# Eight high halves before eight low ones in mixer B, and weight units split in four half-width steps

## The chip, the cores and the metric

The kernel runs on one core of one Trainium2 chip. The metric is the device time of one execution in microseconds (us); the median of three runs of the kernel before is 1575.03 us (1574.35 to 1576.03). Engines are named as in the profile: PE is the matrix array (TensorE), PEld its weight loader, DVE is VectorE, ACT is ScalarE, POOL is GpSimd, SP is the engine that issues most of the DMAs. L12 is line 12 of the kernel before.

## The reference, cut to what matters

Two layers over 1024 tokens of width 1024. Layer 0 has mixer A, attention over a neighbourhood of the token grid; layer 1 has mixer B, grouped-query attention over all tokens. Each layer then projects, adds, and adds a gated per-layer embedding. All of it is float32.

```python
def mixer_b(h, w_in, q_norm_g, k_norm_g, w_out):
    proj = h @ w_in
    q, k, v, gate = jnp.split(proj, [...], axis=-1)
    q = rms_norm(q.reshape(b, s, 16, 64), q_norm_g); k = rms_norm(k.reshape(b, s, 4, 64), k_norm_g)
    q, k = rope(q), rope(k)
    ...
        sc = jnp.einsum('bkgqd,bksd->bkgqs', qb, k) * scale
        pr = jax.nn.softmax(sc, axis=-1)
        return jnp.einsum('bkgqs,bksd->bkgqd', pr, v)     # the products with v
    ...
    return (o * jax.nn.silu(gate)) @ w_out
```

Mixer A has 16 heads; each query there attends to a window of 8 x 16 keys with a relative bias.

## The kernel before, in words

**Numbers in two halves.** Each float32 operand of a product is kept as a high half in the array's reduced format (`fp32r`) and a low half, the rest. A projection takes three products for each 128-row piece: high with high, high with low, low with high (`split3`, L303, recorded at L301 like all matmuls). For v, high and low halves of its 64 columns lie side by side in one 128-column tile `V`, so a product with `V` gives both, and the transposed probabilities come as `PTh` and `PTl`.

**The order of the work** is written out by hand. Mixer A runs head by head, eight steps of 128 queries in each; mixer B runs 128 steps of 128 queries (head, half, t) in four groups of 32. In mixer B a step has the scores (`f_S`: four matmuls, then a minimum on DVE, L1054), the exponential (`f_E`: ACT, L1060), the transposition (`f_T`: twice four transposes on PE, L1070, each four into one PSUM bank `t`; ACT writes `PTh`, L1072, then DVE writes `PTl`, L1073, which frees the bank) and, on every second step, the products with v (`f_AV`, L1078). `psT` has two banks, so the transposes of one step need both `PTl` of the step before. `PTh` and `PTl` each hold two steps (256 columns), and `f_AV` multiplies the eight key blocks of both into a bank `o`, 16 matmuls of 128x256:

```python
                for k in range(NT):
                    v = V[h // 4][:, k]
                    mm(o, v, PTh[:, k], t == 1 and k == 0, False)
                    mm(o, v, PTl[:, k], False, t == 3 and k == NT - 1)
```

In the order of emission `f_AV` of one step stands behind the scores and a projection piece or two and ahead of the next transposition. Mixer A has its own `f_AV` (L676), in which high and low also alternate; the change leaves it alone.

**`mix`** (L334) weaves two lists: the attention items, and `dense` items (pieces of the projections for the next head or group, of the gates, and of the per-layer embedding). After each attention item it calls `pulse`, which is one `WQ.pump()` and one tick of `post`, a list of small steps with due times counted in pulses (for instance the evacuation of `o`, L478 and L442, and the norms of q and k, L313 to L323). Dense items then follow as their share of the cost comes due; they call no pulse.

**The weights** come in 92 units of 128x1024 float32 (`Weights`, L176; the queue is `WQ`). `stage` (L193) issues the load of a unit on SP into one of two `wstage` buffers, two units ahead of the split, and not before `lag` = 3 pumps after the last split. `pump` (L205) takes a unit that has been staged for `age` = 3 pumps, if its pool has room, and splits it: ACT copies the unit to the high half (L216), and DVE subtracts to get the low half (L217). The low half is not emitted at once but kept in `rest`; the next `pump`, or the next `get` of any unit by a dense item, emits it through `settle` (L223). `get` (L228) also splits by force if the unit asked for isn't there yet. ACT, DVE, POOL and SP each execute in the order of emission.

In mixer A the table of relative biases of the next head (`table`, L620) is loaded by SP into `u` (L622), and POOL works on it (L625) ahead of the y products (L512, L513); ACT then makes their high half (L509).

Of the kernel before, what the change touches and what calls it, by code (L numbers as in the profile page):

```python
# [15 lines left out]
AF = mybir.ActivationFunctionType  # L16
ALU = mybir.AluOpType
# [4 lines left out]
NT = 8  # L22
# [131 lines left out]
def trunk(ctx, tc, x, wts, rpb, gains, hgains, mask, rope, out):  # L154
    nc = tc.nc
    sync, act, dve, pool, pe = nc.sync, nc.scalar, nc.vector, nc.gpsimd, nc.tensor
# [19 lines left out]
    class Weights:  # L176
        def __init__(self):
            self.q = []
            self.staged = 0
            self.split = 0  # L180
            self.st = {}
            self.live = {1: 0, 2: 0, 3: 0}
            self.cap = {1: WSLOTS, 2: 0, 3: 0}
            self.alloc = {1: lambda: [wp1.tile([128, 1024], F32R, name=f"w{c}1") for c in "hl"]}
            self.clock = 0
            self.tiles = {}
            self.hold = None
            self.age = AGE
            self.lag = LAG
            self.last = -9  # L190
            self.rest = None

        def stage(self, force=False):  # L193
            if not force and self.clock - self.last < self.lag:
# [9 lines left out]

        def pump(self, force=False):  # L205
            self.clock += 1
            self.settle()
            self.stage(force)
            if self.split >= self.staged:
                return  # L210
            key, pid = self.q[self.split]
            if self.live[pid] >= self.cap[pid] or not (force or self.clock - self.st[key][1] >= self.age):
                return
            s, _ = self.st.pop(key)
            hi, lo = self.alloc[pid]()
            act.activation(hi, s, AF.Copy)  # L216
            self.rest = lambda: dve.tensor_tensor(lo, s, hi, ALU.subtract)  # L217
            self.tiles[key] = (hi, lo, pid)
            self.live[pid] += 1
            self.split += 1  # L220
            self.last = self.clock

        def settle(self):  # L223
            if self.rest:
                self.rest()
                self.rest = None

        def get(self, key):  # L228
            self.settle()
# [12 lines left out]
    WQ = Weights()  # L242
# [57 lines left out]
    def mm(ps, a, b, first, last):  # L300
        pe.matmul(ps, a, b, start=first, stop=last, skip_group_check=True)  # L301
# [251 lines left out]
    def mixer_a():  # L553
        with ExitStack() as es:
# [7 lines left out]
            V = one.tile([128, NT, 4, 128], F32R, name="V")  # L562
# [92 lines left out]
            def f_E(h, j):  # L655
                k0, k1 = near(j)
                n = (k1 - k0 + 1) * 128
                sp, mn = SP[h, j]
                act.activation(sp[:, :n], sp[:, :n], AF.Exp, bias=mn, scale=-1.0, accum_out=RS[h][:, j:j + 1])
# [123 lines left out]
            PTh = ptp.tile([128, NT * 3, 128], F32R, name="PTh")  # L783
            PTl = ptp.tile([128, NT * 3, 128], F32R, name="PTl")
# [14 lines left out]
            def av_and_v(h, kb):  # L799
                fs = [(lambda: f_AV(h, kb), CA[4])]  # L800
                if h % 4 == 3 and h < NH - 1:
                    fs += [(f, 0.0) for f in v_items(h // 4 + 1, kb)]
                return fs

            for h in range(NH):
                att = []
                for j in range(NT):
                    n = h * NT + j
                    def head(h=h, j=j):
                        later.tick()  # L810
                        if j == 1 and h + 1 < NH:
                            table(h + 1)
                    att.append((head, CA[0]))
                    att.append((lambda h=h, j=j: f_T(h, j), CA[1]))
                    if n + 1 < len(steps):
                        att.append((lambda n=n: f_E(*steps[n + 1]), CA[2]))
                    if n + 2 < len(steps):
                        att.append((lambda n=n: f_S(*steps[n + 2]), CA[3]))
                    if n >= 2:
                        att += av_and_v(*steps[n - 2])  # L820
                    if h == 15 and j >= YLOAD_A:
                        for t in ((j - YLOAD_A,) if j < NT - 1 else range(j - YLOAD_A, NT)):
                            att.append((lambda t=t: load_y(0, t), 0.0))
                    if h == 14 and j == OPEN3:
                        att.append((open3, 0.0))
                if h == NH - 1:
                    att += [(lambda: f_AV(NH - 1, NT - 2), CA[4]), (lambda: f_AV(NH - 1, NT - 1), CA[4])]
                dense = []
                if h < NH - 1:
                    dense += qk_items(h + 1)  # L830
                p = h // 2
                if h < 14:
                    dense += gate_items("ag", p, h % 2, dalloc, sb, gg)
                elif h == 14:
                    dense += gate_items("ag", 7, 0, dalloc, sb, gg) + gate_items("ag", 7, 1, dalloc, sb, gg)
                else:
                    dense += pp_items(0, dalloc, sb, TAGS_A)
                mix(att, dense, 4 if h == 0 else 0, HOLD if h == NH - 1 else 0)
            post.flush()
            later.flush()  # L840
            WQ.cap[3] = 0

    def mixer_b(pend):
        with ExitStack() as es:
# [10 lines left out]
            PTh = one.tile([128, NT, 256], F32R, name="PTh")  # L855
            PTl = one.tile([128, NT, 256], F32R, name="PTl")
# [9 lines left out]
            KA, KB, V, QT, QST, P, RS, OP = {}, {}, {}, {}, {}, {}, {}, {}  # L866
# [211 lines left out]
            def f_AV(h, hf, t):  # L1078
                if t == 1:
                    OP[h, hf] = psO.tile([128, 512], F32, name="o")  # L1080
                o = OP[h, hf][:, (t - 1) * 128:(t + 1) * 128]
                for k in range(NT):
                    v = V[h // 4][:, k]
                    mm(o, v, PTh[:, k], t == 1 and k == 0, False)
                    mm(o, v, PTl[:, k], False, t == 3 and k == NT - 1)
                if t == 3:
                    fin = head_end(sb, h, hf, RS[h, hf], OP.pop((h, hf)), ylive, 1, gg, talloc)
                    if fin:
                        later.add(FIN[1], fin)
# [9 lines left out]
            for i, d in enumerate(pre):  # L1099
# [4 lines left out]
                d[0]()  # L1104
                pulse()
            pro[0] = False
            for g in range(4):
                att = []
                for n in range(32 * g, 32 * g + 32):
                    h, hf, t = steps[n]  # L1110
                    av = n >= 2 and n % 2 == 0
                    w = CB if av else CN
                    att.append((later.tick, w[0]))
                    if av:
                        att.append((lambda n=n: f_AV(*steps[n - 1]), w[1]))
                    te = [(lambda n=n: f_T(*steps[n]), w[2])]
                    if n + 1 < len(steps):
                        te.append((lambda n=n: f_E(*steps[n + 1]), w[3]))
                    if n % 2 == 0:
                        te.reverse()  # L1120
                    att += te
                    if n + 2 < len(steps):
                        att.append((lambda n=n: f_S(*steps[n + 2]), w[4]))
                    m = n + QS_AT
                    if m % 8 == 0 and m < len(steps):
                        hn, fn, _ = steps[m]
                        att.append((lambda hn=hn, fn=fn: q_stack(hn // 2, fn), 0.0))
                    if YLOAD_B <= n < YLOAD_B + NT:
                        att.append((lambda t=n - YLOAD_B: load_y(1, t), 0.0))
                if g == 3:  # L1130
                    att.append((lambda: f_AV(*steps[-1]), CB[1]))
                def gates(p):
                    return [i for hf in range(2) for i in gate_items("bg", p, hf, dalloc, sb, gg)]
                dense = []
                if g > 0:
                    dense += left
                if g < 3:
                    qi = q_items(g + 1, pool)
                    kv = kv_items(1, pool) if g == 1 else [None, None]
                    dense += kv[:-2] + qi[:KS] + [k for k in kv[-2:-1] if k] + qi[KS:8] + [k for k in kv[-1:] if k] + gates(2 * g + 1) + qi[8:]  # L1140
                    left = gates(2 * g + 2)
                else:
                    WQ.cap[3] = 2
                    dense += gates(2 * g + 1) + pp_items(1, dalloc, sb, TAGS_B)
                mix(att, dense, hold=HOLD if g == 3 else 0)
            post.flush()
            later.flush()
            WQ.cap[3] = 0

    def dense_phase(l):  # L1150
# [164 lines left out]
```

## Time and profile before

| what | value |
| --- | --- |
| median of three runs | 1575.03 us (1574.35 to 1576.03) |
| the profiled execution, its own time | 1577.5 us |
| its span, first to last instruction | 1575.6 us |
| PE, PEld, DVE, ACT, POOL busy | 1523.6, 1328.7, 1023.9, 871.4, 269.5 us |
| mean granted clock of the array | 0.997 |

The busy times come from the profile's first part. In its groups of instructions a row gives line, engine, operation, tiles, shape, count, then busy time, mean duration in ns of one, and the engine's idle time before them with what ended it. A row of waits gives who waited, for whom, and total, number and longest in us. A row of the busy time by stage gives the stretch in us from the span's start, its length, then busy time and count for PE, PEld, DVE, ACT and POOL, the granted clock, the busy share of the DMA engines, and GB/s. A row of the timeline gives start and duration in us. Matmuls overlap, so their pace is read from one start to the next and not from their durations. A row of the chain that ended last gives start, duration, and what the end then hung on.

### The profile page before, as it was taken

The numbers are of one execution on the slowest core, as the hardware profiler recorded it, in microseconds if no ns is written. First come the engines' busy times: TensorE is split into PE (matmuls) and PEld (weight loads), VectorE is DVE, ScalarE is ACT, GpSimd is POOL, SyncE is SP. The second block draws the span as 40 slices with busy tenths as digits, with TensorE's granted clock in tenths as the row PEclk, the third lists the DMA queues.
The fourth block names the chain that finished last, engine by engine and source line by source line (L and its number), as shares of the span: only waits on it lengthen the run. The fifth ranks groups of instructions, "written<-read, shape, count | busy, mean of one in ns | idle before, by whom it ended". The sixth has DMA issues, their size and how long they took to land.

```text
span 1575.6 us, 24284 instructions
## 1 busy us (share of the span) xinstructions
PE 1523.6 (97%) x9048; PEld 1328.7 (84%) x9048; DVE 1023.9 (65%) x2062; ACT 871.4 (55%) x1744; POOL 269.5 (17%) x372
## 2 busy tenths in 40 slices
PE   6999999999999999999999999999999999999997
PEld 5888988988988788888988889989899888778886
DVE  6566576376467435648877786777777877525636
ACT  6465465366366622433467676766667767622422
POOL 2102102112022010000222132443131200000023
PEclk9999999999999999999999999999999999999999
DMA  8212122132122972142210111102111213651213
GB/s 272 78 45 65 53 80 78 39 92 78 39 79 77 343 257 68 54 140 94 74 49 21 38 51 41 58 24 65 39 32 43 74 41 112 223 201 54 71 55 129
DMA packets 89861, 138.84 MB, mean 88 GB/s; under 512 B 16912, under 2 KB 55952, under 8 KB 89744
## 3 DMA queue, kind: packets, MB, share of 16 engines
q1 hardware_dynamic: 85136, 122.62, 23.8%
q10 hardware_dynamic: 4608, 14.68, 2.6%
q8 instruction: 71, 1.16, 0.3%
q14 instruction: 46, 0.38, 0.1%
HBM read 104.65 MB, written 36.15 MB: 89 GB/s over the span
## 4 chain that ended last, share of the span: by engine, by line
PE 41%; DVE 7%; ACT 3%; issue 2%; ACTq 0%; DVEq 0%
PE d L301 21%; PE o L301 8%; PE t L1070 5%; PE s L301 5%; DVE PTl L1073 2%; DVE mn L1054 1%; ACT PTh L1072 1%; DVE wl L217 1%; PE t L426 1%; ACT wh L216 1%; PE t L1024 0%; ACT P L1060 0%; DVE QS L1034 0%; DVE ss L901 0%; DVE KB L965 0%
## 5 line engine op out<-in xcount | busy, mean ns | idle before, releaser
L301 PE MATMUL d<-wh,HTh 128*128 128x256 f32 (+1 forms) x1096 | 372.3, 340 | 5.0 <-ACT HTh L427 2.3
L301 PE MATMUL d<-wh,HTl 128*128 128x256 f32 (+1 forms) x1096 | 365.8, 334 | 1.5 <-DVE HTl L428 1.5
L301 PE MATMUL d<-wl,HTh 128*128 128x256 f32 (+1 forms) x1096 | 365.2, 333 | 0.0
L1073 DVE TENSOR_TENSOR PTl<-t,PTh 128x512 fp32r<-128x512 f32 x256 | 164.4, 683 | 114.8 <-ACT PTh L1072 114.4
L301 PEld LDWEIGHTS d<-wh,HTh 128*128 128x128 f32 x1096 | 207.7, 189 | 28.3 <-ACT HTh L427 2.9
L301 PEld LDWEIGHTS d<-wh,HTl 128*128 128x128 f32 x1096 | 207.7, 189 | 24.1 <-DVE HTl L428 2.2
L301 PEld LDWEIGHTS d<-wl,HTh 128*128 128x128 f32 x1096 | 208.0, 190 | 21.6
L301 PE MATMUL d<-HTh,wh 128*128 128x512 f32 x504 | 205.9, 409 | 0.0
L301 PE MATMUL d<-HTh,wl 128*128 128x512 f32 x504 | 197.8, 392 | 0.0
L301 PE MATMUL d<-HTl,wh 128*128 128x512 f32 x504 | 197.5, 392 | 0.0
L1060 ACT ACTIVATE P<-s,mn 128x1024 f32<-128x1024 f32 x128 | 142.7, 1114 | 66.6 <-DVE mn L1054 65.7
L301 PE MATMUL o<-PTl,V 128*128 128x256 f32 (+2 forms) x672 | 175.6, 292 | 3.3 <-DVE PTl L1073 2.2
L301 PE MATMUL o<-PTh,V 128*128 128x256 f32 (+2 forms) x672 | 174.2, 289 | 2.6 <-ACT P L1060 1.1
L1072 ACT ACTIVATE PTh<-t 128x512 fp32r<-128x512 f32 x256 | 139.4, 592 | 44.9 <-PE t L1070 44.3
L1054 DVE TENSOR_REDUCE mn<-s 128x1 f32<-128x1024 f32 x128 | 154.7, 1209 | 10.9 <-PE s L301 10.8
L1070 PE MATMUL t<-ident,P 128*128 128x128 f32 x1024 | 136.9, 275 | 7.6 <-DVE PTl L1073 6.1
L217 DVE TENSOR_TENSOR wl<-wstage,wh 128x1024 fp32r<-128x1024 f32 x89 | 113.8, 1284 | 40.8 <-ACT wh L216 40.3
L301 PEld LDWEIGHTS o<-PTl,V 128*128 128x128 f32 x672 | 128.9, 192 | 10.7 <-DVE PTl L1073 6.5
L301 PEld LDWEIGHTS o<-PTh,V 128*128 128x128 f32 x672 | 128.7, 192 | 8.3 <-issue 1.5
L1070 PEld LDWEIGHTS t<-ident,P 128*128 128x128 f32 x1024 | 115.0, 140 | 22.2 <-DVE PTl L1073 15.6
L301 PE MATMUL s<-KA,QS 128*128 128x512 f32 (+2 forms) x384 | 133.6, 402 | 0.0
L301 PE MATMUL s<-KB,QS 128*128 128x512 f32 (+2 forms) x384 | 121.8, 371 | 0.0
(178 smaller groups left out, 2436.9 us busy)
## 6 DMA issues: line engine op xcount, KB each, us to landing
wstage<-in_wts SPq DMA_DIRECT2D x92, 512.0 KB
X<-in_x SPq DMA_DIRECT2D x16, 512.0 KB
pp<-ppD SPq DMA_DIRECT2D x32, 256.0 KB
rb<-rD SPq DMA_DIRECT2D x56, 128.0 KB
ppD<-th SPq DMA_DIRECT2D x24, 256.0 KB
xD<-X SPq DMA_DIRECT2D x8, 512.0 KB
X<-xD SPq DMA_DIRECT2D x8, 512.0 KB
yD0h<-rb SPq DMA_DIRECT2D x14, 256.0 KB
```

Of the source, the lines that this page charges most:

```text
L216: act.activation(hi, s, AF.Copy)
L217: self.rest = lambda: dve.tensor_tensor(lo, s, hi, ALU.subtract)
L301: pe.matmul(ps, a, b, start=first, stop=last, skip_group_check=True)
L426: pe.transpose(ps[:, k], xn[:, (4 * c + k) * 128:(4 * c + k + 1) * 128], ident)
L1054: dve.tensor_reduce(mn, ps, axis=AX.X, op=ALU.min)
L1060: act.activation(p, ps, AF.Exp, bias=mn, scale=-1.0, accum_out=RS[h, hf][:, t:t + 1])
L1070: pe.transpose(ps[:, i], p[:, k * 128:(k + 1) * 128], ident)
L1072: act.activation(PTh[:, ks, c], ps, AF.Copy)
L1073: dve.tensor_tensor(PTl[:, ks, c], ps, PTh[:, ks, c], ALU.subtract)
```

## The change

Two edits. In mixer B's `f_AV` the eight products with `PTh` come first, then the eight with `PTl`. And while `WQ.fine` is set, which it is during the main loops of both mixers, `pump` splits a unit that isn't forced in four steps: high half of columns 0 to 511, high half of columns 512 to 1023 (both ACT), then the two low halves (both DVE). The first step is emitted at once; each later `pump` emits one step and returns, without staging a load and without splitting another unit until none is left. A `get` by a dense item still emits all steps that are left. Outside the main loops the split stays as it was.

```diff
         def pump(self, force=False):
             self.clock += 1
+            if self.fine and self.rest:
+                self.settle(1)
+                return
             self.settle()
             self.stage(force)
...
             hi, lo = self.alloc[pid]()
-            act.activation(hi, s, AF.Copy)
-            self.rest = lambda: dve.tensor_tensor(lo, s, hi, ALU.subtract)
+            ws = (slice(0, 512), slice(512, 1024)) if self.fine and not force else (slice(0, 1024),)
+            for w in ws:
+                self.rest.append(lambda w=w: act.activation(hi[:, w], s[:, w], AF.Copy))
+            for w in ws:
+                self.rest.append(lambda w=w: dve.tensor_tensor(lo[:, w], s[:, w], hi[:, w], ALU.subtract))
+            self.settle(1)
...
-        def settle(self):
-            if self.rest:
-                self.rest()
-                self.rest = None
+        def settle(self, n=9):
+            while self.rest and n:
+                self.rest.pop(0)()
+                n -= 1
...
# mixer_a, ahead of its loop over heads, and mixer_b, ahead of its loop over groups
+            WQ.fine = True
...
# both, behind that loop
             post.flush()
             later.flush()
+            WQ.settle()
+            WQ.fine = False
...
# mixer_b, f_AV
                 for k in range(NT):
-                    v = V[h // 4][:, k]
-                    mm(o, v, PTh[:, k], t == 1 and k == 0, False)
-                    mm(o, v, PTl[:, k], False, t == 3 and k == NT - 1)
+                    mm(o, V[h // 4][:, k], PTh[:, k], t == 1 and k == 0, False)
+                for k in range(NT):
+                    mm(o, V[h // 4][:, k], PTl[:, k], False, t == 3 and k == NT - 1)
```

More of the change, by code (lines that the diff above doesn't have):

```diff
@@ L190, in __init__ @@
             self.last = -9
-            self.rest = None
+            self.rest = []
+            self.fine = False
         def stage(self, force=False):
@@ L221, in pump @@
             self.last = self.clock
-        def settle(self):
-            if self.rest:
-                self.rest()
-                self.rest = None
+        def settle(self, n=9):
+            while self.rest and n:
+                self.rest.pop(0)()
+                n -= 1
         def get(self, key):
@@ L1106, in mixer_b @@
             pro[0] = False
+            WQ.fine = True
             for g in range(4):
@@ L1147, in mixer_b @@
             later.flush()
+            WQ.settle()
+            WQ.fine = False
             WQ.cap[3] = 0
```

## The prediction

> **What bounds the kernel now.** I read the page first, then the busy time by stage, then the waits inside mixer B's loop, then single places on the timeline and the chain that ended last.
>
> ```profile
> span 1575.6 us, 24284 instructions
> PE 1523.6 (97%) x9048; PEld 1328.7 (84%) x9048; DVE 1023.9 (65%) x2062; ACT 871.4 (55%) x1744; POOL 269.5 (17%) x372
> 85.00:546.00 461.00, 453.08 (x2595) 395.75 (x2594) 282.85 (x640) 268.15 (x595) 72.73 (x96) 1.00 0.27 86
> 800.00:1382.00 582.00, 565.29 (x3825) 505.96 (x3823) 430.59 (x686) 406.92 (x755) 135.52 (x213) 1.00 0.19 60
> ```
>
> The last two rows are mixer A's loop and mixer B's loop (length; then busy time of PE, PEld, DVE, ACT, POOL). The matrix array is busy in 98% of A's loop and 97% of B's. So only time in which the array stands still can be won: 461.0 - 453.1 = 7.9 us in A, 582.0 - 565.3 = 16.7 us in B. VectorE (DVE) and ScalarE (ACT) have room on average (74% and 70% in B), so they hurt by lateness at a place and not by their total. Who was late in B, as waits of the array and of its weight loader (total, times, longest):
>
> ```profile
> PEld t L1070 <- DVE PTl L1073: 15.6, 34, 2.0
> PEld o L301 <- DVE PTl L1073: 6.5, 15, 1.0
> PE t L1070 <- DVE PTl L1073: 6.1, 6, 1.6
> PE o L301 <- DVE PTl L1073: 2.2, 7, 0.7
> ```
>
> `PTl`, the low half of the transposed probabilities and DVE's work, is the late tile. The products with v (o, L301) wait for it 15 times, and the transpositions (L1070) wait for it because it frees their PSUM bank. The change attacks the first row directly; its second half touches what makes DVE late.
>
> **Part 1: eight high halves first.** The worst of the 15 waits, products and then DVE:
>
> ```profile
> 932.77 0.28 PE L301 MATMUL o<-PTh,V 128*128 128x256 f32 x1
> 933.77 0.39 PE L301 MATMUL o<-PTl,V 128*128 128x256 f32 x1 [0.72 <-DVE PTl L1073]
> 933.99 0.28 PE L301 MATMUL o<-PTh,V 128*128 128x256 f32 x1
> 934.11 0.28 PE L301 MATMUL o<-PTl,V 128*128 128x256 f32 x1
> ...
> 933.03 1.28 DVE L1073 TENSOR_TENSOR PTl<-t,PTh 128x512 fp32r<-128x512 f32 x2
> ```
>
> Undisturbed products follow each other by 934.11 - 933.99 = 0.12 us. The first low one stood behind one high product and came 1.00 us after it, so 0.88 us were lost. With eight high products ahead it is not due until 8 x 0.12 = 0.96 us after the first, which leaves 0.04 us of this wait. The fifth low product needs the second `PTl`: it is due at 932.77 + 12 x 0.12 = 934.21, and that tile ends at 934.31, so this worst place keeps 0.10 us. All others are shorter and vanish. The loader's total counts the normal step too: 6.5 - 15 x 0.12 = 4.7 us lost now, 0.1 us kept, 4.6 us won on the array. The lower bound is the array's own idle time, 2.2 - 0.1 = 2.1 us.
>
> Nothing is added: 16 products and 16 weight loads before and after, into the same bank. The fifth high product is now due 0.48 us after the first instead of 0.96 us, so the second `PTh` must be there earlier. ACT covers that:
>
> ```profile
> 931.63 1.06 ACT L1072 ACTIVATE PTh<-t 128x512 fp32r<-128x512 f32 x2
> ```
>
> Both are done at 932.69, before the first product starts at 932.77; where that cover is missing it costs up to 0.48 us. The transpositions behind the products are due earlier by what is won, and DVE is not earlier, so a part comes back at their PSUM bank. In place of 4.6 us I take 4.0, nearer the loader's figure because ends on the array are modelled while starts are recorded. Bounds: 1 (nearly all comes back) to 4.6.
>
> **Part 2: a unit in four steps.** Units converted in the two loops now (ACT; first A, then B from 870 us on), and prices:
>
> ```profile
> L216 ACT ACTIVATE wh<-wstage x31: 1041/1051/1063, 76.5 to 545.3; 128x1024 fp32r<-128x1024 f32 x31
> L216 ACT ACTIVATE KA<-wstage x1: 1047/1047/1047, 505.6 to 505.6; 128x1024 fp32r<-128x1024 f32 x1
> L216 ACT ACTIVATE wh<-wstage x17: 1041/1045/1062, 883.9 to 1381.8; 128x1024 fp32r<-128x1024 f32 x17
> L216 ACT ACTIVATE KA<-wstage x2: 1060/1064/1067, 1235.2 to 1236.1; 128x1024 fp32r<-128x1024 f32 x2
> 929.73 1.99 ACT L216 ACTIVATE wh<-wstage 128x1024 fp32r<-128x1024 f32 x2
> L509 ACT ACTIVATE rb<-Y 128x512 fp32r<-128x512 f32 x28 | 17.4, 623 | 12.5 <-POOL Y L513 12.5
> L217 DVE TENSOR_TENSOR wl<-wstage,wh x17: 1210/1218/1340, 885.0 to 1384.1; 128x1024 fp32r<-128x1024 f32 x17
> L510 DVE TENSOR_TENSOR Y<-Y,rb 128x512 fp32r<-128x512 f32 x28 | 20.7, 739 | 7.5 <-ACT rb L509 7.1
> ```
>
> That is 32 units in A and 19 in B; none of them is forced, so all are halved. Cost of halving: on ACT 2 x 0.623 - 1.05 = 0.20 us if nothing overlaps; but a unit right behind another takes only 1.99 - 1.04 = 0.95 us, an overlap of 0.10, and with that on the extra step it is 0.10 us. On DVE 2 x 0.739 - 1.22 = 0.26 us at most; the two `PTl` above take 1.28 us together, 0.06 more than one whole unit. I take 0.10 + 0.06 = 0.16 us a unit, 8 us over 51 units, between 8 and 23. Most of this lies in idle time: in B 19 x 0.16 = 3 us on two engines that idle 151 and 175 us. I charge 0.3 us to the array in B and nothing in A, whose array waits are few and start elsewhere (below); without that cover it is the 3 us.
>
> [...]
>
> The gain is in who stands behind a unit. From the chain that ended last, where units are in it ahead of a stall of the array:
>
> ```profile
> 884.01 0.95 ACT wh L216
> ...
> 1096.08 1.34 DVE wl L217
> 1099.29 1.13 DVE wl L217
> ...
> 1237.80 1.22 DVE KB L217
> 1239.23 1.22 DVE KB L217
> ...
> 1339.71 1.05 ACT wh L216
> ```
>
> and two of the stalls on the array:
>
> ```profile
> 1102.42 1.25 PE L1070 MATMUL t<-ident,P 128*128 128x128 f32 x8 [0.88 <-DVE PTl L1073]
> 1241.40 1.25 PE L1070 MATMUL t<-ident,P 128*128 128x128 f32 x8 [0.72 <-DVE PTl L1073]
> ```
>
> At 1102 and 1241 two units were split on neighbouring pumps and both low halves stood in front of the `PTl` that frees the bank. Now the second unit's first step comes three pumps later, unless a projection in between flushes the first. At 1102 none does in time, by the code, so one low half of 1.1 us leaves the queue ahead of that `PTl`, more than the stall of 0.88 us. At 1241 the first unit is flushed at once and only one half of the second is put off: I take half of 0.72, 0.36 us. At 884 and 1339 the exponential stands behind one ACT half instead of two: 0.45 us each where the pump in between comes in time, 0.9 us. Together at most 0.88 + 0.36 + 0.9 = 2.1 us; the steps that are moved stand in front of something else, which I put at half of that. Part 2 gives 1.1 - 0.3 = 0.8 us won, with bounds of 2.1 won and 3 lost.
>
> In A no stall of the array names a unit. The seven waits of its transpositions are for the exponential:
>
> ```profile
> PE t L667 <- ACT sp L659: 5.7, 7, 1.5
> ...
> 113.13 1.23 DVE L217 TENSOR_TENSOR wl<-wstage,wh 128x1024 fp32r<-128x1024 f32 x1 [0.25 <-ACT wh L216]
> 115.57 1.03 SPq L201 DMA_DIRECT2D wstage<-in_wts  x1
> 116.70 0.36 SPq L622 DMA_DIRECT2D u<-U  x1
> ```
>
> What A risks is the SP queue. The next unit's load waits there until the low half of the unit two before is done (114.36 here), and the bias table `u` waits behind it, then POOL, the y product and the ACT queue. The load reached its place 1.2 us after the low half. The low half now ends later by one or two pumps of some 0.67 us (about 690 pumps in 461 us by the code), so this cover is about used up but not exceeded: nothing taken, at most 1.3 us at each of four such places. Elsewhere the first use of a unit lies at least ten pumps behind its split, by the code, so no product waits for a unit; the last unit of each loop is settled at the loop's end, as now.
>
> **Clock.** Near the end of mixer B the granted clock halves once:
>
> ```profile
> 1374.00:1377.00 3.00, 3.00 (x14) 3.00 (x15) 0.97 (x3) 0.00 (x0) 0.00 (x0) 0.50 0.00 0
> ```
>
> The 14 products there take 3.00 us instead of 14 x 0.12 = 1.7. Whether this stretch stays, goes or moves when the tail shifts the trace cannot say: 1.3 us either way, in the range only.
>
> **Sum.** The profiled execution took 1577.5 us, its span 1575.6; the median of the three runs is 1575.03, 2.5 below the profiled one. -4.0 (part 1) -0.8 (part 2) = -4.8: 1572.7 for such an execution, **1570.2** for the median.
>
> **Rivals.**
> 1. *The wait moves to the bank.* DVE is just as late, so the transpositions behind the products wait instead (the 34 waits above speak for it; that only six stop the array itself speaks against). Part 1 keeps 1 us, part 2 its 0.8: 1573.2.
> 2. *The split does nothing.* Each projection item settles all steps that are left, and one comes every three or four pumps. Then part 2 is only its 0.3 us: 1575.0 - 4.0 + 0.3 = 1571.3. By the code a third of B's units are flushed within one pump, most are not.
> 3. *More stalls (slower).* In B each deferred second low half lands in front of a `PTl` that a transposition is waiting for: 19 x 0.60 = 11.4 us added, less part 1's 4.0: 1582.4. It needs the array's lead over DVE at these places to be under 0.6 us; seven of 19 such hits eat the gain, twelve make it slower by 3.2 us. For it speaks that DVE's lateness already shows in 34 loader waits; against it, that these steps were in the same queue before.
> 4. *A's table.* The four places late by 1.3 us each: +5.2 on the forecast, so 1575.4, no change.
>
> **How the numbers follow.** A difference of 0.2% (3.2 us) is about what can be told from none. Forecast 0.56; rival 1 0.17, rival 2 0.10, rival 3 0.13, rival 4 0.04. Faster: 0.56 + 0.10 = 0.66 (forecast and rival 2, below 1571.9); same: 0.17 + 0.04 = 0.21; slower: 0.13. Low end: part 1 at 4.6, part 2 at 2.1, the clock stretch 1.3, and 2 for stalls of B that I did not trace to a unit: 1565.0. High end: rivals 1, 2 and 4 lie within, and rival 3 up to ten of its hits (19 x 0.60 x 10/19 - 4.0 = +2.0): 1577.0. The upper part of rival 3 and the far lower tail are left out.
>
> **What the profile after would show.** Right: the loader's wait of o for `PTl` in B falls from 6.5 us to under 2, idle time of the array in B's loop from 16.7 to about 12, L216 and L217 rows at 128x512 with twice the count at about 0.62 and 0.70 us, A's loop as long as before. Wrong: the row of L1070 waiting for `PTl` grows by what o loses (rival 1); halves side by side on the timeline (rival 2); new stalls behind 128x512 low halves (rival 3); longer waits of A's transpositions for the exponential (rival 4).

## The result and the profile after

The change made the kernel slower. Its median is 1588.74 us (1586.65 to 1591.37, 6 runs) against 1575.83 us (1574.35 to 1577.3, 6 runs) of the kernel before: a ratio of 1.0085, 95% interval 1.0073 to 1.0098, so 12.9 us more. The forecast was 1570.2 us, with 1565 to 1577 as its range.

The profiled execution took 1589.31 us, its span 1587.5. From its busy time by stage (length; PE, PEld, DVE, ACT, POOL; granted clock; DMA share; GB/s), the first stage as in the prediction, the second moved by the 14.39 us by which mixer B starts its first transposition later:

```profile
85.00:546.00 461.00, 445.45 (x2537) 388.86 (x2536) 275.80 (x657) 263.50 (x611) 71.07 (x95) 0.99 0.24 74
814.39:1393.97 579.58, 562.71 (x3825) 504.72 (x3823) 429.88 (x704) 409.89 (x773) 136.22 (x213) 1.00 0.19 60
```

In A's stretch the array now stands idle for 461.0 - 445.5 = 15.5 us instead of 7.9, and has 2537 of 2595 matmuls behind it: the stage is longer. In B's it stands idle for 579.6 - 562.7 = 16.9 us, as before (16.7), and both executions have one stretch at half clock there (granted clock 0.50; the kernel before at 1374, this one at 907.8, shown below). Where the loops end shows how much. The first projection product behind A's loop, then the one behind B's loop, on the timeline of the kernel before:

```profile
545.43 0.50 PE L301 MATMUL d<-wh,HTh 128*128 128x512 f32 x1 [0.92 <-ACT G L544]
1382.00 0.50 PE L301 MATMUL d<-wh,HTh 128*128 128x512 f32 x1 [0.74 <-ACT th L544]
```

and of the changed one:

```profile
559.56 0.50 PE L309 MATMUL d<-wh,HTh 128*128 128x512 f32 x1 [1.11 <-ACT G L552]
1393.97 0.50 PE L309 MATMUL d<-wh,HTh 128*128 128x512 f32 x1 [0.73 <-ACT th L552]
```

A loses 14.1 us by its end. From 85 us to these ends the array is idle for 7.92 us before and 18.15 after (10.2 more), and busy for 452.51 and 456.41 us (3.9 more). Everything from there to B's end gives back 14.13 - 11.97 = 2.2 us. So the loss lies where the prediction took nothing. The waits of the array and of ACT in A's loop (total, times, longest) name it:

```profile
PE t L675 <- ACT sp L667: 16.6, 7, 3.4
ACT wh L222 <- DMA wstage<-in_wts: 8.6, 3, 3.4
```

The array's wait for the exponential `sp` rose from 5.7 to 16.6 us in the same number of places. The second row is new in the loop: three times ACT itself stood waiting for a weight unit that had not landed. One of the three places, on SP, ACT and PE:

```profile
198.13 1.29 SPq L457 DMA_DIRECT2D rD<-r8T  x4
200.31 1.09 SPq L459 DMA_DIRECT2D rb<-rD  x2
201.50 1.01 SPq L202 DMA_DIRECT2D wstage<-in_wts  x2
...
206.20 1.15 ACT L222 ACTIVATE wh<-wstage 128x512 fp32r<-128x512 f32 x2 [2.26 <-DMA wstage<-in_wts]
...
209.05 0.62 ACT L667 ACTIVATE sp<-sp,mn 128x384 f32<-128x384 f32 x1
...
209.81 0.55 PE L675 MATMUL t<-ident,sp 128*128 128x128 f32 x3 [2.29 <-ACT sp L667]
```

and the same work before:

```profile
193.80 2.57 SPq L201 DMA_DIRECT2D wstage<-in_wts  x2
196.62 1.54 SPq L449 DMA_DIRECT2D rD<-r8T  x4
...
201.37 1.05 ACT L216 ACTIVATE wh<-wstage 128x1024 fp32r<-128x1024 f32 x1
```

The two loads stood ahead of the six small DMAs of the reciprocals (`rD`, `rb`), which wait on SP for DVE and for each other (in A's loop of the changed kernel `rD` for `r8T` 128.2 us in 14 places, `rb` for `rD` 11.7 in 27). Now they stand behind them and start 7.7 us later, where the kernel as a whole is 1.5 us late (`rD` at 198.13 for 196.62). ACT reaches the split, finds nothing, and holds four operations behind it, the last of which is the exponential that the array needs. By the code this happens at three places in A, where two units came due on neighbouring pumps: the second now waits for the first one's steps, the staging behind it waits for its own steps and comes a further pump later, and so it falls past the place where `rD` and `rb` are issued.

### The profile page after: what moved, and what is told of

Its sections match the earlier page's. It is cut to its first block, busy times and chain, and to the rows that moved or that the text cites. A ratio compares the mean times of both kernels' runs of the same rounds, so it can differ in the third digit from the quotient of the medians.

```text
span 1587.5 us, 24377 instructions
## 1 busy us (share of the span) xinstructions
PE 1525.3 (96%) x9048; PEld 1330.3 (84%) x9048; DVE 1021.4 (64%) x2113; ACT 877.5 (55%) x1795; POOL 269.0 (17%) x372
## 4 chain that ended last, share of the span: by engine, by line
PE 42%; DVE 7%; ACT 2%; issue 2%; ACTq 0%; DVEq 0%
PE d L309 22%; PE o L309 8%; PE t L1081 6%; PE s L309 5%; DVE PTl L1084 2%; DVE mn L1065 1%; ACT PTh L1083 1%; ACT P L1071 1%; PE t L434 1%; DVE wl L224 1%; PE t L1035 0%; DVE QS L1045 0%; DVE Y L450 0%; DVE KB L976 0%; DVE ss L912 0%
## 5 line engine op out<-in xcount | busy, mean ns | idle before, releaser
L224 DVE TENSOR_TENSOR wl<-wstage,wh 128x512 fp32r<-128x512 f32 (+1 forms) x137 | 118.0, 883 | 25.4 <-ACT wh L222 25.3
L679 DVE TENSOR_TENSOR PTl<-t,PTh 128x384 fp32r<-128x384 f32 (+1 forms) x128 | 66.6, 520 | 105.4 <-ACT PTh L678 104.3
L309 PE MATMUL o<-PTh,V 128*128 128x256 f32 (+2 forms) x672 | 119.2, 288 | 3.6 <-DVE Y L450 3.3
L309 PE MATMUL o<-PTl,V 128*128 128x256 f32 (+2 forms) x672 | 120.0, 290 | 0.3 <-DVE PTl L679 0.3
L309 PEld LDWEIGHTS d<-HTh,wl 128*128 128x128 f32 x504 | 95.2, 189 | 21.9
```

The source lines that it names most:

```text
L224: self.rest.append(lambda w=w: dve.tensor_tensor(lo[:, w], s[:, w], hi[:, w], ALU.subtract))
L679: dve.tensor_tensor(PTl[:, sl], ps[:, :m], PTh[:, sl], ALU.subtract)
```

## Experiments

Ratios are to the kernel before on the same chip (medians 1574.39, 1575.14 and 1575.39 us). Theory S, formed from the trace above: the loss is the order on SP, not the halving. Its rival, theory H: the halved steps themselves cost. In the later texts P is S made wider (the place at which steps and loads stand, in B too), and U is about the bias table.

### a1: the order of v's products alone

The edit is the last part of the diff, put on the kernel before.

> The kernel before with the products with v reordered in mixer B and nothing else. In the profile of the change mixer B's loop is about 2.4 us shorter while mixer A's is about 14 us longer. If the reorder does what the prediction worked out, the waits of the low products for PTl vanish and the kernel is 3 to 5 us faster than before (about 1571.5). If the wait only moves to the transpositions' PSUM bank, it is within 1.5 us of before.

Measured: 1571.51 us (1570.58 to 1573.38), ratio 0.9981, interval 0.9972 to 0.9990: 2.9 us faster. Waits in B's loop:

```profile
PEld t L1070 <- DVE PTl L1073: 21.2, 48, 2.0
PE t L1070 <- DVE PTl L1073: 7.4, 9, 1.6
```

No row of `o` waiting for `PTl` is left, on either side. The loader's wait of the transpositions rose by 5.6 us, from 15.6 in 34 places to 21.2 in 48, nearly as much as the `o` row lost (6.5); but only 1.3 of it stops the array (6.1 to 7.4). The reorder does what it says, and part of it comes back at the bank.

### a2: the split in mixer B alone

The kernel before with the new `Weights`, and `WQ.fine = True` only ahead of B's loop; old order of v's products.

> The kernel before with the four half-width steps in mixer B's loop alone, the old order of products. Theory S (the loss comes from the order of loads on the SP queue in mixer A): B's loop has no such place, so this is within 3 us of before, most likely 1 to 2 us slower, since the change's gain of 2.4 us in B is less than the reorder's 4. Theory H (half-width steps make ScalarE and VectorE late wherever they are): 19 of the 51 units are here, so 19/51 of some 17 us, 5 to 7 us slower than before.

Measured: 1577.41 us (1574.61 to 1581.48), ratio 1.0021, interval 1.0010 to 1.0031: 3.0 us slower, between the likely figures of the two expectations. The profiled execution took 1581.48 us, 4 us above the median; it has two stretches at half clock ahead of its end (0.50 from 542 to 544 and from 1255 to 1258), the first of them where the code is that of the kernel before. S's premise that B has no such place does not quite hold either: near 1245 ACT waits 1.54 us for a weight unit whose load started at 1243.71, where the kernel before started it at 1240.47.

### c1: the split in mixer A alone

The same with `WQ.fine = True` only ahead of A's loop.

> The kernel before with the split of the change in mixer A's loop alone: B's units are whole, and v's products are in the old order. If the three parts of the change add up (order of v's products -2.9 us, split in B +3.0, the change +12.9 in all), this gives 1586.5 to 1589.5, +12 to +14 us, all of it before the end of A's loop. The rival, that the parts work on each other (the split in A is cheaper by itself and B's parts lose more together than alone), expects under 1584.

Measured: 1589.07 us (1584.06 to 1591.29), ratio 1.0076, interval 1.0063 to 1.0088: 13.7 us slower by the medians, 12.0 by the ratio, so this part alone is about as slow as the whole change. In its trace, of an execution of 1591.29 us, the array waits 15.4 us for the exponential in A, in seven places.

The parts add up within their intervals: by the ratios 0.76 + 0.21 - 0.19 = 0.78%, where the change cost 0.85% (0.73 to 0.98).

### a3: whole units, loads one pump later

No unit is split; only the staging in A's loop comes a pump later.

```diff
+            WQ.lag = 4
             for h in range(NH):
...
+            WQ.lag = LAG
             post.flush()
```

> The kernel before, unsplit and with the old order of products, but in mixer A's loop a unit is staged four pumps after the last split instead of three. At three places that puts two weight loads on SP behind the four rD and two rb transfers, as the change does there. Theory S: stalls of A's transpositions of 2.4 to 3.6 us near 210, 337 and 466 us as in the change, 8 to 11 us slower than before (1584 to 1587). Theory H: no step is halved, so within 1 us of before.

Measured: 1590.37 us (1589.03 to 1594.56), ratio 1.0105, interval 1.0091 to 1.0118: 16 us slower with not one step halved, more than the 8 to 11 us that theory S had expected. Timeline of SP and ACT at the first place:

```profile
195.86 1.29 SPq L449 DMA_DIRECT2D rD<-r8T  x4
...
199.23 1.01 SPq L201 DMA_DIRECT2D wstage<-in_wts  x2
...
204.15 1.06 ACT L216 ACTIVATE wh<-wstage 128x1024 fp32r<-128x1024 f32 x1 [3.43 <-DMA wstage<-in_wts]
```

and the array's wait in A's loop:

```profile
PE t L667 <- ACT sp L659: 13.6, 11, 3.9
```

The same order on SP and the same wait on ACT as in the change. The loads start 5.4 us later than in the kernel before (199.23 for 193.80), far more than the one pump, since they now stand behind `rD` and `rb`. The three long waits of the array are 3.4, 3.2 and 3.9 us, in place of 2.3, 3.5 and 2.9 in the change, while those near 130, 255 and 380 are gone. Each of the three comes here with a stretch at half clock (0.50 from 207 to 213, 337 to 339 and 463 to 466): to the end of A's loop the array is idle for 7.7 us more than before and busy for 6.1 us more, which an expectation made from the stalls alone left out. Theory S holds: loads that fall behind `rD` and `rb` are enough to make a loss of this size.

### a4: the whole change, loads one pump earlier

The change with `WQ.lag = 2` at the same two places.

> The whole change, but in mixer A's loop a unit is staged two pumps after the last split instead of three, so that at those three places the first of the two weight loads is issued ahead of the rD and rb transfers again; the half-width steps stay. Theory S: the three stalls of 2.4 to 3.6 us go, 8 to 11 us faster than the change (1578 to 1581). Theory H: the steps are as many and as late as in the change, so 1587 to 1590.

Measured: 1579.36 us (1577.62 to 1580.17), ratio 1.0027, interval 1.0015 to 1.0038: of the change's 0.85%, 0.58 are gone (9 us), with every unit still in four steps. Its trace has the first of the two loads back ahead of `rD` (197.49 against 198.08), ACT's wait in the loop is gone, and the array keeps three waits:

```profile
PE t L675 <- ACT sp L667: 5.8, 3, 2.5
```

### b2 and b3: the bias table loaded earlier

The three waits left (near 129.9, 254.5 and 378.0 us) are places where the kernel before had shorter ones. The chain before, on DVE, SP, ACT and PE:

```profile
111.77 0.21 DVE L446 STREAM_TRANSPOSE r8T<-r 128x32 f32<-128x32 f32 x1
...
116.70 0.36 SPq L622 DMA_DIRECT2D u<-U  x1
...
127.06 0.63 ACT L509 ACTIVATE rb<-Y 128x512 fp32r<-128x512 f32 x1 [4.08 <-POOL Y L513]
128.72 0.33 PE L667 MATMUL t<-ident,sp 128*128 128x128 f32 x1 [1.24 <-ACT sp L659]
```

and after:

```profile
112.84 0.21 DVE L454 STREAM_TRANSPOSE r8T<-r 128x32 f32<-128x32 f32 x1
...
118.43 0.36 SPq L630 DMA_DIRECT2D u<-U  x1
...
128.26 0.63 ACT L517 ACTIVATE rb<-Y 128x512 fp32r<-128x512 f32 x1 [5.37 <-POOL Y L521]
129.91 0.48 PE L675 MATMUL t<-ident,sp 128*128 128x128 f32 x1 [2.56 <-ACT sp L667]
```

The delay starts on DVE (the low halves now stand in front of `r8T`, 1.1 us), passes over SP to `u` (1.7 us), from there over POOL's table and y products to ACT (1.2 us), and reaches the array as 1.2 us. If so, loading `u` earlier cuts the chain. Both kernels issue it four steps sooner, one on the change with lag 2, the other on the kernel with the new order of v's products and whole units:

```diff
+            def load_u(h):
+                UU[h] = sb.tile([128, 16, 24], F32, name="u", bufs=1)
+                sync.dma_start(UU[h], U2[h].rearrange("p (r c) -> p r c", r=16))
             def table(h):
-                u = sb.tile([128, 16, 24], F32, name="u", bufs=1)
-                sync.dma_start(u, U2[h].rearrange("p (r c) -> p r c", r=16))
+                u = UU.pop(h)
...
                             table(h + 1)
+                        if j == 5 and h + 2 < NH:
+                            load_u(h + 2)
```

> The change with the staging lag of 2 in A's loop (1579.36), and the table's load u issued four steps earlier on SP (at step 5 of the head before, instead of right ahead of POOL's work on it). Theory U (the three waits of 2.6, 1.7 and 1.9 us left in A come through r8T, rD and rb ahead of the stage, u behind it on SP, POOL's table and Y, and ACT's rb ahead of the exponential) expects two thirds or more of these 6.2 us to go: 1574 to 1575.5. The rival (they come from the halved steps in ACT's and DVE's own queues) expects 1578.5 to 1580.

> The kernel before with the order of v's products of the change, unsplit (1571.51 when it was run alone), and u's load issued four steps earlier as in the run with u early. Theory U expects the three waits of 1.4, 1.4 and 1.6 us that the kernel before has in A to go for the most part, 3 to 4 us less: 1567.5 to 1568.5. The rival expects 1571 to 1572.

Measured: b2 1573.24 us (1570.97 to 1574.19), ratio 0.9986, interval 0.9977 to 0.9995; b3 1567.99 us (1567.12 to 1569.54), ratio 0.9956, interval 0.9945 to 0.9968. By their ratios b2 is 6.5 us better than a4, a little more than theory U's range, and b3 is 3.9 better than a1, as expected. The array's wait for the exponential in A, first in b2, then in b3:

```profile
PE t L680 <- ACT sp L672: 1.1, 3, 0.8
```

```profile
PE t L672 <- ACT sp L664: 0.5, 3, 0.2
```

So these waits did come through `u`. b3, whole units with the new order and an early table, is the best version found: 6.9 us faster than the kernel before, 20 us faster than the change.

### b1: halves without the spreading

Both loops with half-width steps, but both high halves issued at once and both low ones at the next pump, and nothing held back for them; old order of v's products.

> The kernel before, with every converted unit of both mixers' loops in four half-width steps, but without the spreading: both high halves are issued at the pump at which the whole step was, both low halves at the next one, and no staging waits for them. The order of v's products is the old one. Theory P (position: the change loses through where its steps and the loads behind them stand, not through their width) expects the time of the kernel before within 1 us (1573.4 to 1575.4): 51 units times some 0.16 us is 8 us of ACT and DVE time, nearly all beside TensorE. Theory H (the doubled number of steps is the price) expects 2 to 8 us more, 1576.5 to 1582.5, with the exponential's wait in A's loop longer than 5.7 us in sum.

Measured: 1577.30 us (1575.64 to 1581.1), ratio 1.0015, interval 1.0007 to 1.0023: 2.2 us slower, so theory P's "within 1 us" was wrong and the figure is in theory H's range. But H's place was wrong: A's loop ends at 545.59, 0.16 us later than before, with 5.1 us of waits for the exponential instead of 5.7. There the halving is free. In B the delay grows place by place. Before:

```profile
930.98 1.30 DVE L217 TENSOR_TENSOR wl<-wstage,wh 128x1024 fp32r<-128x1024 f32 x1
932.21 0.41 DVE L901 TENSOR_REDUCE ss<-t 128x4 f32<-128x256 f32 x1
...
933.77 0.39 PE L301 MATMUL o<-PTl,V 128*128 128x256 f32 x1 [0.72 <-DVE PTl L1073]
1371.78 0.33 PE L1070 MATMUL t<-ident,P 128*128 128x128 f32 x1 [1.04 <-DVE PTl L1073]
```

with the halves:

```profile
931.47 1.92 DVE L220 TENSOR_TENSOR wl<-wstage,wh 128x512 fp32r<-128x512 f32 x2
933.32 0.41 DVE L907 TENSOR_REDUCE ss<-t 128x4 f32<-128x256 f32 x1
...
934.79 0.39 PE L304 MATMUL o<-PTl,V 128*128 128x256 f32 x1 [1.22 <-DVE PTl L1079]
1373.71 0.33 PE L1076 MATMUL t<-ident,P 128*128 128x128 f32 x1 [1.04 <-DVE PTl L1079]
```

From the low half's start to the next operation DVE needed 1.23 us before and 1.85 us here (one of the two halves took 1.23 us by itself; why, the trace does not show), and `PTl` behind it holds the array 0.5 us longer. Late by 1.02 us at 933.77 (0.46 of it were there at the products at 891), the array is late by 1.93 us at 1371.78. So halving alone costs about 1.5 us of array time over B's 19 units in this pair of executions.

### b4: whole units, the low half one pump later in B

No unit is split; the low step in B's loop waits one pump more.

```diff
             self.clock += 1
+            if self.late and self.rest and self.clock - self.last < 2:
+                return
             self.settle()
```

> The kernel before, unsplit, with the low step of a weight unit in mixer B's loop issued two pumps after the high one instead of one. Theory P expects what splitting alone in B cost, +1.5 to +3.5 us (1576 to 1578): the 1.23 us step leaves DVE's idle time before PTl and stands behind it, in the run ahead of the next Y and PTl, so that PE's waits for DVE near 885 and 1350 grow by about 1 us each. Theory H expects the time of the kernel before (1573.6 to 1575.2), since no step is halved.

Measured: 1576.83 us (1573.97 to 1579.8), ratio 1.0010, interval 1.0002 to 1.0019: 1.7 us slower, as theory P said. (The new `return` also puts a second unit that is due on the next pump back by one.) But the trace bears out only half of the reason. DVE before a stall of the products with v, in the kernel before:

```profile
885.00 1.23 DVE L217 TENSOR_TENSOR wl<-wstage,wh 128x1024 fp32r<-128x1024 f32 x1 [0.26 <-ACT wh L216]
887.09 1.29 DVE L1073 TENSOR_TENSOR PTl<-t,PTh 128x512 fp32r<-128x512 f32 x2 [0.87 <-ACT PTh L1072]
...
891.15 0.36 PE L301 MATMUL o<-PTh,V 128*128 128x256 f32 x1 [1.12 <-ACT P L1060]
```

and with the late low half:

```profile
887.78 1.29 DVE L1076 TENSOR_TENSOR PTl<-t,PTh 128x512 fp32r<-128x512 f32 x2 [2.35 <-ACT PTh L1075]
888.99 1.22 DVE L220 TENSOR_TENSOR wl<-wstage,wh 128x1024 fp32r<-128x1024 f32 x1
...
892.98 0.36 PE L304 MATMUL o<-PTh,V 128*128 128x256 f32 x1 [2.26 <-DVE Y L445]
```

with the busy time of the stretch right behind it:

```profile
893.90:897.30 3.40, 3.40 (x18) 3.40 (x18) 2.64 (x4) 1.21 (x2) 0.00 (x0) 0.51 0.27 77
```

The low half leaves the time in which DVE waits for ACT anyway (0.26 + 0.87 us, now 2.35) and stands behind `PTl`, in the run that ends with the `Y` for which the products wait: 1.1 us more, here and again near 1347. Elsewhere other waits shrank by as much (those at 933.77, 1102 and 1241 are gone). The last row is a stretch at half clock right behind the long stall. It is not the net loss either: the kernel before has such a stretch at 1374, and from B's first transposition to the end of its loop the two executions take 581.6 and 581.3 us. So this trace does not show where the 1.7 us lie. The granted clocks on record point to such stretches: their mean is 0.99692 over the twelve runs of b4 and 0.99776 over the 29 of the kernel before, which is an estimated 1.3 us of 1577.

## Why the prediction was wrong

**The step that failed** is the one sentence on A, "A's loop as long as before", with "nothing taken" for the SP queue. The price of one stall was looked at through one example place and one cover (the load's wait for the low half). What was not followed was the pump's new `return`: it holds back not only the steps of a unit but the staging of the next loads, and on SP these start behind whatever was emitted ahead of them (at 201.50, right behind `rb`, in the trace above). The prediction named this queue and the chain behind it (rival 4: `u`, POOL, the y product, the ACT queue, then the exponential), priced it at 1.3 us in each of four places and gave it 0.04. The runs showed six places, not four. In three the chain was rival 4's from `u` on, but `u` was late for another reason than the load's wait for a low half: `r8T`, and the DMAs behind it, came later (above). The one shown grew by 1.3 us, just rival 4's price, which is luck: the other two grew by 0.6 and 1.0, and at the fourth place, near 498, the wait of 1.2 us went away. In the other three the loads changed places with `rD` and `rb`, and the wait went straight through ACT's split; beside the 2.29 us at 209.81 these are

```profile
336.94 0.33 PE L675 MATMUL t<-ident,sp 128*128 128x128 f32 x1 [3.45 <-ACT sp L667]
465.71 0.33 PE L675 MATMUL t<-ident,sp 128*128 128x128 f32 x1 [2.88 <-ACT sp L667]
```

The array's waits for the exponential give 16.6 - 5.7 = 10.9 of A's 14.1 us, and 8.6 of these 10.9 are the three places at which the loads moved. Other waits shrank by 0.7. The rest, the 3.9 us for which the array is busy longer, is for the most part what two stretches at half clock take, which A did not have before. In the second, products of 128x512 follow each other by 0.43 us (338.23 to 338.66), behind it by 0.23 (341.44 to 341.67), so a busy array loses an estimated 3.4 x (1 - 0.23 / 0.43) = 1.6 us in each:

```profile
129.60:133.00 3.40, 3.09 (x9) 2.61 (x10) 1.33 (x4) 3.36 (x8) 1.53 (x1) 0.50 0.51 154
337.80:341.20 3.40, 3.40 (x13) 2.91 (x11) 3.26 (x8) 1.93 (x5) 0.00 (x0) 0.50 0.55 190
```

**Part 1** was right in its mechanism and somewhat too large: -4.0 forecast, -2.9 measured alone (a1, interval -1.6 to -4.4). The `o` rows vanished, as worked out. What came back at the bank was sized too small: 1.3 us more on the array's own row, where 0.6 had been taken off.

**Part 2 in B** had the wrong sign: -0.8 forecast, +3.0 measured (a2). The price of an extra step was right where two halves run back to back: 1.15 us on ACT for a pair at 206.20 against 1.05 for a whole unit, the 0.10 that was taken. On DVE a pair took 1.28 us against 1.22 (1239.53 in b1, 1237.80 before), the 0.06 that was taken; at one place in B it was 0.6 more (1.85 for 1.23 us, from 931.47 in b1). But charging 0.3 us of this price to the array, since DVE idles on average, was wrong: the units stand where DVE is late, and b1 shows about 1.5. a2 as a whole came out at the low end of the stated bounds, 3 us lost. The gains expected at 884 and 1339 turned round: the exponential no longer stood behind a whole unit, but the low halves moved into the run ahead of `Y`, and in the split alone (a2) these are the stalls:

```profile
893.81 0.36 PE L309 MATMUL o<-PTh,V 128*128 128x256 f32 x1 [2.32 <-DVE Y L450]
1254.78 0.31 PE L1034 MATMUL t<-ident,qt 128*128 128x128 f32 x1 [2.18 <-DVE PTl L1083]
1351.54 0.33 PE L469 MATMUL o<-ident,rb 128*128 128x128 f32 x1 [2.30 <-DVE Y L450]
```

where before the array had stood for 1.12, 0.85 and 1.01 us. At the second a low half of 1.43 us (1252.61) stands right in front of the `PTl`. At 1102 the transposition's wait of 0.88 us is gone in a2, but the products with v there wait 0.43 us for `Y` and then again for `PTl`, so nothing was won.

**Rivals.** What rival 1 feared came in part: 5.6 of the loader's 6.5 us moved to the bank, but only 1.3 of them stop the array. Rival 3 gave the right side for B and a fair mechanism, far too large (19 hits; three clear ones). Rival 4 had three of the six places, at which the waits grew by 2.9 of the 10.9 us. Of the signs listed as right, two came (no wait of `o` for `PTl`; half-width rows of L222 and L224 at 0.62 and 0.68 us in B) and two did not: B's idle time stayed at 16.9 us, and A's loop grew. Of those listed as wrong, the longer waits for the exponential, the new stalls behind low halves and halves side by side (in A the pair at 206.20 is one of many) came.

**Left open.** Which stalls are followed by a stretch at half clock, and how exactly a2's 3.0 us divide between the halving, the place of the low halves and such stretches. The mean granted clocks of the runs give an estimate: 0.99650 over the eight of a2 against 0.99775 over the 20 of the kernel before is some 2.0 us, while b1's 0.99758 against 0.99776 is 0.3 of its 2.2 us. These means also hold the last microseconds of the span, in which the array has little to do (no matmul from 1569 us on in the kernel before, at a granted clock of 0.50), so they give the direction rather than the size.

## What to carry to other kernels

A helper that spreads one step over several calls also delays everything that it does after that step: list what each early `return` holds back, DMA issues first, and look in the trace at what those issues are moved past on their queue. Here the loads were hidden while they stood ahead of the small dependent DMAs, and not behind them (at the first place ACT waited 2.26 us for them in the change, 3.43 in a3); one slot of the schedule cost 16 us (a3), where the reorder won 2.9 (a1). In B, work that fell into DVE's idle time was best left whole and where it was (in halves the kernel was 2.2 us slower, b1; one pump later 1.7, b4); "this engine idles 30%" says nothing of the places at which its work would be put instead.

## What was not expected of the hardware

Some short stalls cost more than their length here. In the trace of b4 a stall of 2.26 us, in a loop in which the array is otherwise busy in 97% of the time, was followed by 3.4 us at a granted clock of 0.51, and in the changed kernel the one of 3.45 us at 336.94 by the stretch at 337.8 shown above; yet the stalls of 2.30 us at 1351.54 in a2 and of 2.88 us at 465.71 in the changed kernel were not. One and the same stall, of the products with v for `Y` early in B, took 2.32 or 2.33 us in four traces. In the changed kernel half clock followed:

```profile
906.75 0.36 PE L309 MATMUL o<-PTh,V 128*128 128x256 f32 x1 [2.33 <-DVE Y L450]
907.80:911.20 3.40, 3.40 (x19) 3.40 (x18) 2.51 (x4) 1.45 (x3) 0.00 (x0) 0.50 0.36 107
```

In a2 (893.81), a4 (895.07) and b2 (889.32) the clock stayed at 1.00 behind it. So the length of a stall does not decide it alone. What else decides it, these traces do not show.
